# Eight stores of prepared W_out sums, begun on ScalarE's DMA queue in place of SyncE's

## The chip, the cores and the metric

The kernel runs on one core of one Trainium2 chip. The metric is the device time of one execution in microseconds (us); lower is better. A core has TensorE (PE, matrix products), VectorE (DVE), ScalarE (ACT), GpSimd (POOL) and SyncE (SP, which only begins transfers and waits). Each engine takes its own instructions strictly in order; between engines they wait on semaphores. A transfer is begun by an instruction of an engine and then runs by itself.

## The reference, cut to what matters

One decoder layer on a prompt of 2048 tokens and on 8 single decode tokens, all in float32:

```
h = rmsnorm(x, norm_g)
rq, rk, rv, rg, hq, hf, hi, hgate = split(h @ w_in, 8)      # 1024 -> 8 x 512
rq, rk = rotary(rq), rotary(rk) * 128**-0.5                 # 4 retention heads of 128
o_ret, s_ret = chunked_decay_recurrence(rq, rk, rv, log_gamma, s_ret)
logf = logaddexp(log(lb), log1p(-lb) + log_sigmoid(hf))     # 4 HGRN2 heads of 128
kin  = (1 - lb) * sigmoid(-hf)
o_hg, s_hg = chunked_decay_recurrence(silu(hq), kin, hi, logf, s_hg)
o = concat(head_rmsnorm(o_ret) * silu(rg), head_rmsnorm(o_hg) * silu(hgate))
y = rmsnorm(x + o @ w_out)                                  # w_out: 1024 x 1024
```

Returned are y for prompt and decode tokens and all new states. The recurrence is S_t = diag(f_t) S_(t-1) + k_t v_t^T, o_t = S_t^T q_t.

## The kernel before, in words

**Number format.** A float32 product is made of three products of a shorter format: each operand is split into a high part h (a rounded copy, made on ACT, line 115) and a low part l (the rest, made on DVE, line 116), and PE adds h·h, h·l and l·h. `hi_lo` does the two steps; `split` (line 118) does them for a 128x1024 tile, into a tile of the tag `wh` and one of the tag `wl`, of which there are three buffers each. Weights of `w_in` (w0, w1, ... in the order of use) and the sums of `w_out` share these six buffers.

**Stages.** The first 572 us make six of the eight projections and the retention heads, with block products that need fewer multiplications (seven for eight). From there to about 860 us run eight units, one for each half of the prompt and each HGRN2 head: a unit's PE work is the projection to the forget gate (`pjfh`) and to the query (`pjqh`), line 1039, in segments of up to 512 tokens. Between those matmuls PE does the recurrence of the unit before: scores (`pah`, line 1273; `plh`), transposed keys (`pkh`, line 1118), state updates (`puh`), outputs (`poh`, `poth`). The last stage multiplies by `w_out`: four token blocks plainly, the rest with the seven-product form, which needs sums of blocks of `w_out`.

**The path from a query segment to the scores.** When `pjqh` of a segment is complete, ACT makes its sigmoid (`qsh`, line 1095), DVE multiplies (`qqh`, line 1096) and multiplies by the gate (line 1098); the score matmuls `pah` read the result. `pkh` is copied out of PSUM by ACT (`ksh`, line 1120).

**The prepared sums.** Four times, beside units 0, 1, 2 and 4, a row block of `w_out` is loaded (`t_load_raw`), four sums are made on DVE (`t_sum`, lines 1365 to 1371), two of them are stored as they are (`t_keep`), and the other two, side by side in a 128x1024 tile, are split (`t_spool`; tiles `wos0h`, `wos0l` to `wos3h`, `wos3l`) and both parts are stored to DRAM (`t_store`, line 1383). They are read back near 900 us. The places come from a list of fractions of a unit (lines 1445 to 1449).

**What sets the order.** PE's order is as written. The instructions of the other engines are put in order by the layer that builds the program, by its own estimate of when each can start; it also hands out the buffers of a tag, and a new tile waits for the last use of the buffer that it gets, a store out of it among them. Transfers of SP and ACT count on eight counters in turn (`DMAHW0` to `DMAHW7`), and one that takes a counter waits until the transfer before it on that counter has landed. All stores of line 1383 are begun by SP, as nearly all other loads and stores are; ACT begins one transfer in the program, near the end (line 1774).

The lines that begin the stores, and when (as fractions of a unit behind 0.35, 1.35, 2.35 and 4.35):

```
def t_store(k):
    for x, y in zip("hl", tspl[k]):
        sp.dma_start(t_dram[x][:, :, k], ...)
steps += [t_spool, t_keep, t_store]
for f, d in zip(steps, (0, 0.12, 0.18, 0.24, 0.3, 0.4, 0.42, 0.54)):
```

Of the kernel before, what the change touches and what calls it, by code (L numbers as in the profile page):

```python
# [10 lines left out]
F32 = mybir.dt.float32  # L11
# [30 lines left out]
def step_kernel(ctx, tc, a, out):  # L42
    nc = tc.nc
    pe, act, dve, pool, sp = nc.tensor, nc.scalar, nc.vector, nc.gpsimd, nc.sync
# [1300 lines left out]
    def collect(h, u):  # L1345
# [3 lines left out]
    t_dram = {  # L1349
        x: dr.tile([P, 2, 4, GW], F32, tag=f"t{x}", name=f"t_dram{x}") for x in "hlr"  # L1350
    }
# [28 lines left out]

    def t_store(k):
        for x, y in zip("hl", tspl[k]):
            sp.dma_start(t_dram[x][:, :, k], y.bitcast(F32).rearrange("p (a b) -> p a b", a=2))

    def d_norm():
        x = pools["tp"].tile([8 * NB, P], F32, tag="dgt", name="do", bufs=2)
# [605 lines left out]
```

## Time and profile before

| what | value |
|---|---|
| three runs | 1034.69, 1038.95, 1041.99 us; median 1038.95 |
| the profiled execution | 1036.22 us, of which its span is 1034.4 |
| granted TensorE clock | 0.999 |
| PE busy in the span | 1017.0 us (98%) |
| DVE, ACT, POOL busy | 746.1 (72%), 559.2 (54%), 128.7 (12%) us |
| PE busy from 575 to 830 us | 251.7 of 255 us |
| busy share of the DMA engines, 658 to 670 us | 0.79 |

The time that hangs on line 1383 lies between 590 and 745 us of the span. Rows of the time line give start, duration, engine, line, operation, output and inputs (buffer numbers left out), and in brackets how long the engine stood idle ahead of it and for whom. `SPq` and `ACTq` are rows of instructions that begin transfers; their duration is the time in which the engine is held, not that of the transfer.

### The profile page before, as it was taken

What the parts mean: (1) busy time and instruction counts of PE and PEld (TensorE: products, weight loads), DVE (VectorE), ACT (ScalarE), POOL (GpSimd) and SP (SyncE); (2) the same over time, 40 slices, a digit from 0 to 9 for tenths busy, and PEclk for the clock granted to TensorE, in tenths of its full rate; (3) what the DMA queues carried; (4) which work ended last, traced back from release to release, by engine and by line L of the source; (5) the groups of instructions that cost most, each with busy time, mean ns of one, the idle gap of its engine ahead of it and who ended that gap; (6) DMA issues with size and microseconds to landing.
All of it is one profiled execution on the core that took longest, in us unless ns stands there. A gap on an engine that the chain in (4) does not pass through costs nothing.

```text
span 1034.4 us, 21591 instructions
## 1 busy us (share of the span) xinstructions
PE 1017.0 (98%) x8359; PEld 843.5 (82%) x8359; DVE 746.1 (72%) x1387; ACT 559.2 (54%) x1233; POOL 128.7 (12%) x231
## 2 busy tenths in 40 slices
PE   8999999999999999999999999999999999999997
PEld 7777878887778888878888889798788877888775
DVE  6886676887666876666666767768778676667786
ACT  7863346644445765545554756666556465443242
POOL 0410001000000111111111200110012102312122
PEclk9999999999999999999999999999999999999999
DMA  8699999779998974486775696745784395576652
GB/s 292 218 332 335 336 327 318 267 252 321 318 335 296 376 245 156 163 266 220 239 247 175 229 331 226 244 136 195 231 263 136 118 380 196 177 274 210 236 169 102
DMA packets 151271, 255.63 MB, mean 247 GB/s; under 512 B 11424, under 2 KB 79280, under 8 KB 151040
## 3 DMA queue, kind: packets, MB, share of 16 engines
q1 hardware_dynamic: 143584, 229.22, 65.3%
q0 software_dynamic: 7440, 24.76, 6.2%
q8 instruction: 66, 1.08, 0.4%
q14 instruction: 37, 0.30, 0.1%
q10 hardware_dynamic: 144, 0.26, 0.1%
HBM read 166.51 MB, written 87.69 MB: 246 GB/s over the span
## 4 chain that ended last, share of the span: by engine, by line
PE 78%; DMA 11%; ACT 5%; DVE 3%; issue 1%; SPq 1%; POOL 0%; POOLq 0%; ACTq 0%; DVEq 0%
PE po L360 11%; PE pjfh L1039 7%; PE pjqh L1039 6%; PE py L1670 4%; DMA xn<-in_x_prompt 2%; PE plh L1255 2%; PE par L744 1%; PE pur L751 1%; PE por L757 1%; PE por L759 1%; DMA or<-o_dram 1%; DMA T3l<-ws1T 1%; DMA a_dram<-xr 1%; PE puh L1126 1%; PE poh L1142 1%
## 5 line engine op out<-in xcount | busy, mean ns | idle before, releaser
L1235 ACT ACTIVATE kepth<-kh 128x1024 f32<-128x1024 f32 x24 | 25.5, 1061 | 70.7 <-DVE kh L1225 70.7
L1039 PE MATMUL pjfh<-xh,w_h 128*128 128x512 f32 (+2 forms) x160 | 59.6, 372 | 0.8 <-ACT fxh L1087 0.8
L1039 PE MATMUL pjqh<-xh,w_h 128*128 128x512 f32 (+2 forms) x160 | 59.0, 369 | 0.0
L1039 PE MATMUL pjqh<-xh,w_l 128*128 128x512 f32 (+2 forms) x160 | 55.7, 348 | 0.0
L1039 PE MATMUL pjfh<-xh,w_l 128*128 128x512 f32 (+2 forms) x160 | 55.7, 348 | 0.0
L1039 PE MATMUL pjqh<-xl,w_h 128*128 128x512 f32 (+2 forms) x160 | 55.6, 348 | 0.0
L1039 PE MATMUL pjfh<-xl,w_h 128*128 128x512 f32 (+2 forms) x160 | 55.6, 348 | 0.0
L1225 DVE TENSOR_TENSOR kh<-kh,fph 128x512 f32<-128x512 f32 x48 | 33.3, 693 | 18.4 <-PE plh L1255 12.6
L116 DVE TENSOR_TENSOR ab_l<-xr,ab_h 128x512 fp32r<-128x512 f32 (+1 forms) x40 | 37.3, 952 | 5.8 <-ACT ab_h L115 5.8
L782 DVE SCALAR_TENSOR_TENSOR obr<-por,omr,rg 128x128 f32<-128x128 f32 x64 | 18.0, 343 | 32.4 <-POOL omr L774 30.1
L772 ACT ACTIVATE obr<-por 128x128 f32<-128x128 f32 x64 | 16.9, 278 | 43.8 <-PE por L759 41.5
L115 ACT ACTIVATE ab_h<-xr 128x512 fp32r<-128x512 f32 (+1 forms) x40 | 32.4, 841 | 12.5 <-DVE xr L313 12.5
L419 ACT ACTIVATE vo<-vo 128x512 f32<-128x512 f32 x32 | 20.1, 629 | 27.0 <-DVE vo L413 13.7
L1039 PEld LDWEIGHTS pjfh<-xh,w_h 128*128 128x128 f32 x160 | 30.2, 189 | 5.3 <-ACT fxh L1087 1.1
L1039 PEld LDWEIGHTS pjqh<-xh,w_h 128*128 128x128 f32 x160 | 30.4, 190 | 4.8 <-issue 1.2
L1039 PEld LDWEIGHTS pjqh<-xh,w_l 128*128 128x128 f32 x160 | 30.1, 188 | 4.1
L1039 PEld LDWEIGHTS pjfh<-xh,w_l 128*128 128x128 f32 x160 | 30.1, 188 | 4.1
L1228 DVE TENSOR_TENSOR qqh<-qqh,fph 128x512 f32<-128x512 f32 x48 | 32.8, 683 | 0.0
L1039 PEld LDWEIGHTS pjqh<-xl,w_h 128*128 128x128 f32 x160 | 30.2, 189 | 2.9
L1039 PEld LDWEIGHTS pjfh<-xl,w_h 128*128 128x128 f32 x160 | 30.2, 189 | 2.7
L313 DVE SCALAR_TENSOR_TENSOR xr<-xr,g_in,rb 128x256 f32<-128x256 f32 x64 | 27.1, 479 | 6.6 <-issue 4.1
L1670 PE MATMUL py<-woh,oc_h 128*128 128x512 f32 x64 | 26.7, 417 | 1.6 <-issue 1.6
(1840 smaller groups left out, 3371.4 us busy)
## 6 DMA issues: line engine op xcount, KB each, us to landing
xr<-a_dram SPq DMA_DIRECT2D x24, 512.0 KB, 5.6
S<-s_dram SPq DMA_DIRECT2D x24, 512.0 KB, 6.4
xn<-in_x_prompt SPq DMA_DIRECT2D x32, 256.0 KB, 3.6
xr<-in_x_t SPq DMA_DIRECT2D x16, 512.0 KB, 5.9
a_dram<-xr SPq DMA_DIRECT2D x16, 512.0 KB, 4.3
s_dram<-S SPq DMA_DIRECT2D x16, 512.0 KB
wgr<-in_w SPq DMA_DIRECT2D x16, 512.0 KB, 8.2
xr<-a_dram SPq DMA_DIRECT2D x32, 256.0 KB, 4.4
```

The lines of the kernel that those rows point to most:

```text
L115: act.activation(h, src, AF.Copy)
L116: dve.tensor_tensor(l, src, h.bitcast(F32), op=ALU.subtract)
L313: dve.scalar_tensor_tensor(r[:, k], r[:, k], g_in[:, kk : kk + 1], spread_to[i], op0=ALU.mult, op1=ALU.mult)
L360: pe.matmul(ps, xx, ww, start=(first and n == 0), stop=(last and n == 2), skip_group_check=more)
L419: act.activation(o, src, AF.Silu)
L782: dve.scalar_tensor_tensor(o[:, cc], po[:, h], ms[:, h : h + 1], rb_of[c, "g"][:, cc], op0=ALU.mult, op1=ALU.mult)
L1039: pe.matmul(ps, ww[:, kk], x[:, k, b0 : b0 + n], start=(k == 0 and i == 0), stop=(k == KT - 1 and i == 2),)
L1225: dve.tensor_tensor(kv[:, :, 0, :], kv[:, :, 0, :], two[:, :, 1:2].to_broadcast([P, nb, b]), op=ALU.mult)
L1228: dve.tensor_tensor(qv[:, :, 1, :], qv[:, :, 1, :], two[:, :, 0:1].to_broadcast([P, nb, b]), op=ALU.mult)
L1235: act.activation(ss[:, 512:], k[:, :HALF], AF.Copy)
L1255: pe.matmul(dst[32 * i : 32 * i + 32, c], kk, qq, start=True, stop=True)
L1670: pe.matmul(ps, o[:, kk], w[:, k % 4, i * 512 : (i + 1) * 512], start=(k == 0 and n == 0), stop=(k == KT - 1 and n == 2),)
```

## The change

The two stores of each prepared block are begun by ScalarE. Nothing that is computed changes, and the bytes moved are the same.

```
 def t_store(k):
     for x, y in zip("hl", tspl[k]):
-        sp.dma_start(t_dram[x][:, :, k], y.bitcast(F32).rearrange("p (a b) -> p a b", a=2))
+        act.dma_start(t_dram[x][:, :, k], y.bitcast(F32).rearrange("p (a b) -> p a b", a=2))
```

The building layer then places other instructions anew. PE's and POOL's order stays; ACT has eight rows more, SP eight fewer.

On ACT at the third pair (unit 2), before; `w7_h` is the high part of the weights that unit 3's query projection uses, and in brackets are the counters it waits for:

```order
L1095 ACTIVATE qsh02512_6842<-pjqh02_512_6767 128x256 [waits PE_49]
L115 ACTIVATE w7_h_6964<-wr7_6962 128x1024 [waits DMAHW7_49,DMAHW5_49,DVE_49]
L1120 ACTIVATE ksh010_6872<-pkh010_6867 128x512 [waits PE_49]
L1120 ACTIVATE ksh011_6885<-pkh011_6880 128x512 [waits PE_49]
L1095 ACTIVATE qsh02768_6887<-pjqh02_768_6846 128x264
```

The same place on ACT, with the change:

```order
L1095 ACTIVATE qsh02512_6842<-pjqh02_512_6767 128x256 [waits PE_49]
L1383 DMA t_dramh_5499<-wos2h_6831 256x1x512 [waits DMAHW1_49,Activation_49]
L1383 DMA t_draml_5500<-wos2l_6832 256x1x512 [waits DMAHW3_49,DVE_49]
L1120 ACTIVATE ksh010_6872<-pkh010_6867 128x512 [waits PE_49]
L1120 ACTIVATE ksh011_6885<-pkh011_6880 128x512 [waits PE_49]
L1095 ACTIVATE qsh02768_6887<-pjqh02_768_6846 128x264
L115 ACTIVATE w7_h_6964<-wr7_6962 128x1024 [waits DMAHW5_49,DMAHW2_49]
```

The copy to `w7_h` has gone from ahead of the last query sigmoid of the unit to behind it. Its buffer is another too: before it was that of `wos2h`, and its wait on `DMAHW7` is for the store `t_dramh<-wos2h`; now it is that of `w5_h`, and `DMAHW2` stands for the store of `w5_h` to DRAM, begun a unit earlier. The first store waits on ACT for the store of `w6_l` (`DMAHW1`), the second for a load of `xr` (`DMAHW3`) and for DVE's `wos2l`.

On DVE at the same place (difference; - before, + with the change):

```order
-L116 TENSOR_TENSOR w7_l_6965<-wr7_6962,w7_h_6964 128x1024
 L1216 TENSOR_TENSOR fph02_6894<-fph02_6894 128x64
-L1096 TENSOR_TENSOR qqh02_6420<-pjqh02_768_6846,qsh02768_6887 128x264
 L1216 TENSOR_TENSOR fph02_6894<-fph02_6894 128x32
-L1098 TENSOR_TENSOR qqh02_6420<-qqh02_6420,fh02_6418 128x256
-L1347 COPY dq_173<-qqh02_6420 128x8
 L1216 TENSOR_TENSOR fph02_6894<-fph02_6894 128x16
 L1216 TENSOR_TENSOR fph02_6894<-fph02_6894 128x8
 L1218 COPY dech02_6902<-fph02_6894 128x8
+L1096 TENSOR_TENSOR qqh02_6420<-pjqh02_768_6846,qsh02768_6887 128x264
+L1098 TENSOR_TENSOR qqh02_6420<-qqh02_6420,fh02_6418 128x256
+L1347 COPY dq_173<-qqh02_6420 128x8
```

The low part `w7_l` follows that last row now, ahead of line 1225. Units 0 and 1 change alike: the last query segment goes ahead of the copy of the next weights, on ACT and on DVE.

On ACT at the fourth pair (unit 4; difference):

```order
 L1319 ACTIVATE Ah_5664<-Abh03_7498 32x8x32 x2
+L1383 DMA t_dramh_5499<-wos3h_7895 256x1x512
 L1314 ACTIVATE Ah_5664<-plh035_7919 32x4x32 x4
 L1316 ACTIVATE Ah_5664<-plh035_7919 64x4x64 x2
-L1095 ACTIVATE qsh10512_7992<-pjqh10_512_7906 128x512
+L1383 DMA t_draml_5500<-wos3l_7896 256x1x512
 L1120 ACTIVATE ksh030_7983<-pkh030_7978 128x512
 L1120 ACTIVATE ksh031_7990<-pkh031_7985 128x512
+L1095 ACTIVATE qsh10512_7992<-pjqh10_512_7906 128x512
```

Here the query sigmoid goes back, behind both stores and both copies of `ksh`.

## The prediction

> **What bounds the kernel now.** I read the page's first part, then who PE waits for in the stretch of the stores, then the chain of waits there, then the time line engine by engine.
>
> ```profile
> PE 1017.0 (98%) x8359; PEld 843.5 (82%) x8359; DVE 746.1 (72%) x1387; ACT 559.2 (54%) x1233; POOL 128.7 (12%) x231
> ```
>
> PE is busy for 1017.0 of 1034.4 us. Only what fills a gap of PE, or opens one, moves the time. Its waits between 575 and 830 us, where the stores lie:
>
> ```profile
> PE pah L1273 <- DVE qqh L1098: 1.6, 1, 1.6
> PE pjfh L1039 <- ACT fxh L1087: 0.8, 1, 0.8
> ```
>
> One gap there is longer than a microsecond. The chain of waits names its cause:
>
> ```profile
> 659.50 6.49 DMA t_dramh<-wos2h
> 666.09 1.07 ACT w_h L115
> 667.19 1.23 DVE w_l L116
> ```
>
> A store of the changed line is on the chain, 6.49 us from issue to landing, because ACT's next weight copy takes the buffer that it empties. On ACT, with what is queued behind:
>
> ```profile
> 661.59 0.39 ACT L1095 ACTIVATE qsh<-pjqh 128x256 f32<-128x256 f32 x1
> 666.09 1.06 ACT L115 ACTIVATE w_h<-wr 128x1024 fp32r<-128x1024 f32 x1 [4.11 <-DMA t_dramh<-wos2h]
> 667.06 1.06 ACT L1120 ACTIVATE ksh<-pkh 128x512 f32<-128x512 f32 x2
> 668.01 0.39 ACT L1095 ACTIVATE qsh<-pjqh 128x264 f32<-128x264 f32 x1
> ```
>
> ACT stands for 4.11 us in front of `w7_h`; behind that copy wait two key copies and the last query sigmoid. DVE and PE follow:
>
> ```profile
> 660.89 1.22 DVE L116 TENSOR_TENSOR wos2l<-wot,wos2h 128x1024 fp32r<-128x1024 f32 x1
> 668.92 0.42 DVE L1098 TENSOR_TENSOR qqh<-qqh,fh 128x256 f32<-128x256 f32 x1
> 669.90 0.69 DVE L1225 TENSOR_TENSOR kh<-kh,fh 128x512 f32<-128x512 f32 x1
> ```
>
> ```profile
> 663.71 0.60 PE L1118 MATMUL pkh<-ident,kh 128*128 128x128 f32 x4
> 666.98 0.88 PE L1273 MATMUL pah<-qqh,kh 128*32 128x64 f32 x48
> 669.40 0.43 PE L1273 MATMUL pah<-qqh,kh 128*32 128x64 f32 x16 [1.55 <-DVE qqh L1098]
> 669.76 0.50 PE L1039 MATMUL pjfh<-xh,w_h 128*128 128x512 f32 x1
> ```
>
> `pah` does 48 of its 64 matmuls, waits for the last query segment, and the projection goes on 2.78 us after `pah` began (669.76 - 666.98). The same step in unit 1 finds its data there:
>
> ```profile
> 631.78 1.10 PE L1273 MATMUL pah<-qqh,kh 128*32 128x64 f32 x64
> 632.81 0.50 PE L1039 MATMUL pjfh<-xh,w_h 128*128 128x512 f32 x1
> ```
>
> That takes 632.81 - 631.78 = 1.03 us.
>
> **The third pair: the gap.** With the change ACT no longer has `w7_h` ahead of the query sigmoid, and `w7_h` has a buffer that does not wait for this store. In its place ACT begins the two stores. What an issue costs an engine:
>
> ```profile
> L1383 SPq DMA_DIRECT2D t_draml<-wos2l x1: 729/729/729, 662.1 to 662.1; - x1
> L1383 SPq DMA_DIRECT2D t_dramh<-wos3h x1: 519/519/519, 731.9 to 731.9; - x1
> L1774 ACTq DMA_DIRECT2D out_y_prompt<-xro x1: 395/395/395, 1030.9 to 1030.9; - x1
> L156 SPq DMA_DIRECT2D w_h<-w_kepth x8: 332/864/4045, 668.9 to 789.1; - x8
> ```
>
> The same stores held SP 0.52 to 0.73 us; ACT's only issue, half as large, 0.40. The last row is the upper bound: an issue can hold SP 4.05 us, though that was a load. I take 0.52 for each, from the same stores, and 0.73 where the queue is busy, as here. The second store needs `wos2l`, ready at 660.89 + 1.22 = 662.11, and the `xr` load that had its counter before:
>
> ```profile
> 650.99 0.33 SPq L173 DMA_DIRECT2D w_keptl<-w_l  x1
> 652.21 7.08 SPq L186 DMA_DIRECT2D xr<-a_dram  x4
> ```
>
> ```profile
> xr<-a_dram SPq DMA_DIRECT2D x32, 256.0 KB, 4.4
> ```
>
> That is the first of the four loads, begun at 652.21; with 4.4 us it lands near 656.6, with the 6.49 of the slow store at 658.7. The first store's counter was held by the store of `w6_l`, begun at 650.99, which is gone sooner still. So on the clock of the old trace ACT is free at 661.59 + 0.39 = 661.98, has begun both stores by 661.98 + 2 x 0.73 = 663.44, copies the second keys after 663.71 + 0.60 = 664.31 until 664.9, and ends the sigmoid (0.39) at 665.3. In the old trace line 1098 ended (668.92 + 0.42 = 669.34) 0.94 us after its sigmoid (668.40); now that is 666.24. PE needs it at 666.98 + 0.88 = 667.86. The margin is 1.6 us, `pah` runs through in 1.03 instead of 2.78, and PE gains **1.75 us** (at the least the 1.55 in brackets).
>
> What is late next? `w7_h` runs from 665.3 to 666.4, and `w7_l` (1.23) on DVE until about 667.6, ahead of line 1225. That line waits for the end of `pah`, at 666.98 + 1.03 = 668.0, so 0.4 us of cover is left; without it line 1225 would start later by what is missing, as would the scores behind it. SP loses a wait and gets one:
>
> ```profile
> 668.86 0.41 SPq L156 DMA_DIRECT2D w_h<-w_kepth  x1
> ```
>
> This load now waits on SP for the store begun on ACT, about 662.5 + 6.49 = 669.0, and holds the value loads behind it as long as before. I cost that at nothing.
>
> **The fourth pair: a cost.** Here ACT's query sigmoid goes back.
>
> ```profile
> 733.38 1.11 ACT L1314 ACTIVATE Ah<-plh 32x128 f32<-32x128 f32 x4
> 734.50 0.77 ACT L1316 ACTIVATE Ah<-plh 64x256 f32<-64x256 f32 x2
> 735.99 0.60 ACT L1095 ACTIVATE qsh<-pjqh 128x512 f32<-128x512 f32 x1 [0.72 <-PE pjqh L1039]
> 736.49 1.08 ACT L1120 ACTIVATE ksh<-pkh 128x512 f32<-128x512 f32 x2
> ```
>
> ```profile
> 737.35 0.69 DVE L1098 TENSOR_TENSOR qqh<-qqh,fh 128x512 f32<-128x512 f32 x1
> ```
>
> ```profile
> 703.42 0.39 SPq L156 DMA_DIRECT2D w_l<-w_keptl  x1
> 703.86 0.42 SPq L1066 DMA_DIRECT2D v<-v_dram  x1
> ```
>
> ```profile
> 739.51 1.10 PE L1273 MATMUL pah<-qqh,kh 128*32 128x64 f32 x64
> ```
>
> The loads whose counters the two stores take were begun near 703.4 and 703.9, 30 us earlier. The first store moves line 1316's end from 735.27 to 735.79, the second lasts until 736.31; the key copies end between 737.4 and 737.6, the sigmoid 0.60 later, at 738.0 to 738.2. Line 1098 ended 1.45 us after it (738.04 - 736.59), so now at 739.45 to 739.65, while `pah` is due at 739.51. That is between nothing and 0.15 us; I take 0.05. All cover is used up here: each further microsecond that ACT is held costs PE one. With the upper bound of 4.05 for one of the issues the loss is 3.5 us.
>
> **The first two pairs.** At unit 0 the sigmoid stood behind a weight copy of a microsecond, which it now has behind it, with the stores in its place.
>
> ```profile
> 598.69 0.51 ACT L1089 ACTIVATE kh<-fxh,lb 128x264 f32<-128x264 f32 x1
> 600.60 0.37 ACT L1095 ACTIVATE qsh<-pjqh 128x264 f32<-128x264 f32 x1
> ```
>
> Two issues from 599.20 end at 600.24, so it is not later than the old 600.60. At unit 1 the second store waits on ACT for `wos1l`, and the key copies and the sigmoid wait behind it:
>
> ```profile
> 627.19 1.23 DVE L116 TENSOR_TENSOR wos1l<-wot,wos1h 128x1024 fp32r<-128x1024 f32 x1 [0.54 <-ACT wos1h L115]
> 629.74 0.38 ACT L1095 ACTIVATE qsh<-pjqh 128x264 f32<-128x264 f32 x1
> ```
>
> The store ends at 628.42 + 0.52 = 628.94, the key copies (1.08) at 630.0, the sigmoid at 630.4 instead of 630.12. The low part of the weights, which DVE did ahead of the query, now follows it, so `pah` at 631.78 still finds its query. Both pairs count as nothing, with 0.3 us either way.
>
> **The sum.** -1.75 + 0.05 = -1.7 us. The profiled execution took 1036.22 us (span 1034.4), which gives 1034.5. The median of the three runs is 1038.95, 2.7 above that execution, and they spread from 1034.69 to 1041.99. From the median I predict **1037.2 us**, 0.16% faster. A change of about 1% is what a measurement of this kernel can tell from none.
>
> **The rivals.** *The gain is given back* (chance 0.22). PE comes to 670 us earlier, but a later wait grows by as much: the 0.8 us for `fxh`, or one in the last stage that hangs on a transfer and not on PE. Against it: between 670 and 830 us PE has only small gaps. The time is 1036.2 on the profile, 1038.95 as a median. The Trainium skill (DMA: Bandwidth & Descriptors, Issuing engines are not separate DMA queues) says that transfers begun by several engines interleave on the same 16 DMA engines, and that only issue time on the sequencer is saved. By that rule alone the change would bring nothing, since SP's issue time bounds nothing here; the trace neither shows nor denies it, having hardly a transfer of ACT's. My gain does not rest on faster stores: it comes from what no longer stands behind one.
>
> *ScalarE is held while it begins a store* (0.10). Place: the fourth pair. If one issue there takes the 4.05 us of SP's longest, PE waits 3.5 us and the result is -1.75 + 3.5 = +1.8: 1040.7, slower than before. It turns the sign from 1.7 us of extra holding on. At the third pair the first 1.6 us are free. Against it: these very stores never took over 0.73 on SP.
>
> *More is gained* (0.10). SP is free of eight issues, the loads behind them start sooner, and the 0.8 us wait for `fxh` goes too: -1.75 - 0.84 = -2.6, so 1036.4.
>
> **How the numbers follow.** The forecast has the remaining 0.58. The cases give 1036.4 to 1040.7; the runs shown scatter by 4.3 below and 3.0 above their median, more than the cases differ, and a new median moves with them. So 1033 to 1042 should hold it. No case comes near 1%; only scatter or something unseen could: faster 0.03, within 1% 0.94, slower 0.03.
>
> **What would show it.** Right: in unit 2 no idle time ahead of `pah`, all 64 in one row, ACT's `w_h` behind `qsh` without a wait for `t_dramh<-wos2h`, and two ACTq rows of 0.4 to 0.75 us. At unit 4 `pah` waits at most 0.2 us for line 1098. Wrong: ACTq rows of more than a microsecond, a wait of `pah` for line 1098 in unit 4, or a longer wait of PE near 700 or 855 us.

## The result, and the profile after

The changed kernel took 1037.24 us and the kernel before 1039.78 us beside it (medians of 22 and 21 runs); the ratio is 0.9977, with a 95% interval of 0.9968 to 0.9987. By the prediction's bound of 1% that is no change; by the interval it is 1.3 to 3.3 us faster. Two further sets, of 11 and 12 runs, gave 0.9977 (0.9961 to 0.9993) and 0.9992 (0.9976 to 1.0009). Forecast were 1037.2 us and a gain of 1.7 us, a ratio of 0.9983, which all three intervals hold. Left out everywhere are four runs of 1440 to 3579 us: one of before, two of the fourth pair in halves, and one of the changed kernel's second set, the profiled one, at a granted clock of 0.655 from end to end, so that this profile isn't read.

The profiled execution of the change was the longest of its 22 (1041.4 us, span 1039.6), that of before one of the shorter (1036.22, span 1034.4). Their spans can't be set against each other; what can is the start of the same PE instruction in both. By how much it is later in the changed kernel is called the lag here. It is 2.6 to 2.7 us from 560 to 608 us (lost in the part before), a constant 2.00 us from 611 to 667, 0.24 us at 669 and 0.20 from 674 to 727. At the third pair the changed kernel has gained 1.76 us; at 610 us it has gained 0.63.

The page, first part, of the changed kernel, and who PE waits for longest between 575 and 830 us (total, times, longest):

```profile
PE 1020.8 (98%) x8359; PEld 845.4 (81%) x8359; DVE 747.7 (72%) x1387; ACT 559.5 (54%) x1233; POOL 129.1 (12%) x231
```

```profile
PE pjfh L1039 <- issue: 2.2, 1, 2.2
PE pjfh L1039 <- ACT fxh L1087: 0.8, 1, 0.8
```

The wait of `pah` for line 1098 is gone, the 0.8 us for `fxh` stands as before, and a stop of 2.2 us is new, in which PE waits for nothing that the profile shows. The time line of the changed kernel at the third pair, ACT first, then DVE and PE:

```profile
662.63 0.52 ACTq L1383 DMA_DIRECT2D t_dramh<-wos2h  x1
664.14 0.52 ACTq L1383 DMA_DIRECT2D t_draml<-wos2l  x1
...
666.84 0.39 ACT L1095 ACTIVATE qsh<-pjqh 128x264 f32<-128x264 f32 x1
667.11 1.06 ACT L115 ACTIVATE w_h<-wr 128x1024 fp32r<-128x1024 f32 x1
```

```profile
667.73 0.43 DVE L1098 TENSOR_TENSOR qqh<-qqh,fh 128x256 f32<-128x256 f32 x1
670.14 0.69 DVE L1225 TENSOR_TENSOR kh<-kh,fh 128x512 f32<-128x512 f32 x1 [0.71 <-PE pah L1273]
```

```profile
668.97 1.10 PE L1273 MATMUL pah<-qqh,kh 128*32 128x64 f32 x64
670.00 0.50 PE L1039 MATMUL pjfh<-xh,w_h 128*128 128x512 f32 x1
```

`w_h` (the tile `w7_h` of the order above) stands behind the query sigmoid and has no bracket: it waited for nothing. Line 1098 ends at 668.16, 0.8 us before `pah` begins, and all 64 matmuls are one row: 1.03 us from `pah` to the projection, where there were 2.78. The fourth pair, ACT and then PE:

```profile
731.92 0.52 ACTq L1383 DMA_DIRECT2D t_dramh<-wos3h  x1
...
733.38 0.55 ACT L1314 ACTIVATE Ah<-plh 32x128 f32<-32x128 f32 x2
733.72 0.52 ACTq L1383 DMA_DIRECT2D t_draml<-wos3l  x1
...
734.50 0.77 ACT L1316 ACTIVATE Ah<-plh 64x256 f32<-64x256 f32 x2
736.43 1.09 ACT L1120 ACTIVATE ksh<-pkh 128x512 f32<-128x512 f32 x2 [1.16 <-PE pkh L1118]
737.41 0.60 ACT L1095 ACTIVATE qsh<-pjqh 128x512 f32<-128x512 f32 x1
```

```profile
739.51 1.10 PE L1273 MATMUL pah<-qqh,kh 128*32 128x64 f32 x64
```

`pah` isn't delayed. Lines 1314 and 1316 start at 733.38 and 734.50 as in the trace of before: an issue of 0.52 us stands on ACT's queue at the same time as an activation, and moves none. Then the new stop, with what follows it on PE:

```profile
752.80 0.50 PE L1039 MATMUL pjfh<-xh,w_l 128*128 128x512 f32 x1 [2.16 <-issue]
...
753.79 0.63 PE L1144 MATMUL poh<-sth,qqh 128*128 128x128 f32 x2
```

Pairs of `poh` take 0.63 us here and 0.39 elsewhere: the granted clock is 0.50 for 3.4 us behind the stop (from 753.35). Between 748 and 760 us the lag grows by 4.0 us.

Open after this trace were two things: whether the third pair is the whole cause, and whether the stop at 752 us belongs to the change.

### The profile page after: what moved, and what is told of

It reads as the page before. It is cut to its first block, busy times and chain, and to the rows that moved or that the text cites. A ratio compares the mean times of both kernels' runs of the same rounds, so it can differ in the third digit from the quotient of the medians.

```text
span 1039.6 us, 21590 instructions
## 1 busy us (share of the span) xinstructions
PE 1020.8 (98%) x8359; PEld 845.4 (81%) x8359; DVE 747.7 (72%) x1387; ACT 559.5 (54%) x1233; POOL 129.1 (12%) x231
## 4 chain that ended last, share of the span: by engine, by line
PE 77%; DMA 12%; DVE 5%; ACT 3%; issue 2%; SPq 1%; POOL 0%; POOLq 0%; ACTq 0%; DVEq 0%
PE po L360 11%; PE pjfh L1039 8%; PE pjqh L1039 7%; PE py L1670 4%; DMA wgr<-in_w 2%; PE plh L1255 2%; PE pur L751 1%; PE por L757 1%; DMA T3l<-ws1T 1%; PE poh L1142 1%; DMA xn<-in_x_prompt 1%; DMA or<-o_dram 1%; PE por L759 1%; PE par L744 1%; PE puh L1126 1%
## 5 line engine op out<-in xcount | busy, mean ns | idle before, releaser
L1670 PE MATMUL py<-wol,oc_h 128*128 128x512 f32 x64 | 25.2, 394 | 2.9 <-issue 2.1
```

What stands on the lines that cost most here:

```text
L1670: pe.matmul(ps, o[:, kk], w[:, k % 4, i * 512 : (i + 1) * 512], start=(k == 0 and n == 0), stop=(k == KT - 1 and n == 2),)
```

## The experiments

**The third pair alone.**

```
-            sp.dma_start(t_dram[x][:, :, k], ...)
+            (act if k == 2 else sp).dma_start(t_dram[x][:, :, k], ...)
```

> Only the third pair's stores are begun on ScalarE. Theory (the gain is the weight copy that no longer stands in front of the query sigmoid at the third pair): the 64 matmuls of pah in unit 2 stand in one row with no idle time ahead of line 1098, 1.75 us are gained, ratio to before 0.9983 (0.9975 to 0.9990). Rival 1 (part of the gain comes from the other pairs, the trace of the changed kernel showed about 0.7 us at unit 0 and 0.2 near 700 us): the ratio is 0.7 to 0.9 us worse than that of the whole change, and unit 0 keeps its idle row of 0.45 us ahead of plh. Rival 2 (the gain is SyncE's freed queue): ratio about 0.9995.

Ratio 0.9971 (0.9954 to 0.9987), median 1036.37 us: better than the 0.9975 to 0.9990 expected, most of which the interval holds. Instructions at 680 us begin 1.79 us sooner against those at 640 than in the trace of before. PE's longest waits in the trace of the third pair alone, 575 to 830 us, have no `pah`:

```profile
PE pjfh L1039 <- ACT fxh L1087: 0.8, 1, 0.8
PE plh L1255 <- issue: 0.8, 1, 0.8
```

The third pair's stores bring at least what all eight do; rival 1 falls as far as the time goes, though its mark in the trace is there (a stop ahead of `plh` in unit 0, here of 0.75 us). Rival 2's 0.9995 lies outside the interval. There is no stop at 752 us.

**All pairs but the third.**

```
+            (sp if k == 2 else act).dma_start(t_dram[x][:, :, k], ...)
```

> The first, second and fourth pair's stores are begun on ScalarE, the third pair's on SyncE as before. Theory: the weight copy of unit 2 again waits about 4 us for the first store, pah stands 1.5 us for line 1098, and the ratio is 1.000 (0.999 to 1.0005). Rival 1: 0.7 to 0.9 us are gained without the third pair, ratio 0.9992, and the 0.45 us idle ahead of plh in unit 0 is gone. Rival 2 (SyncE's freed queue): about three quarters of the gain, ratio 0.9983.

Ratio 0.9991 (0.9977 to 1.0005), median 1038.84 us. The gap is back, on ACT and on PE in the trace of this kernel:

```profile
665.83 1.06 ACT L115 ACTIVATE w_h<-wr 128x1024 fp32r<-128x1024 f32 x1 [3.96 <-DMA t_dramh<-wos2h]
```

```profile
669.14 0.43 PE L1273 MATMUL pah<-qqh,kh 128*32 128x64 f32 x16 [1.39 <-DVE qqh L1098]
```

At the third pair the theory holds in the trace. Rival 1's mark is there as well: the 0.45 us ahead of `plh` in unit 0 is gone, and from 605 to 680 us this kernel gains 0.7 us on the trace of before; by 870 us it has lost 1.3 again. The interval holds nothing gained and also rival 1's 0.9992, so the time alone doesn't decide about the other three pairs.

**Another queue, but the old place of the copy.**

```
+            pool.dma_start(t_dram[x][:, :, k], ...)
```

> All eight stores are begun on GpSimd's queue; in the third pair the next weight copy still takes the buffer that the first store empties, and stands ahead of the query sigmoid. Theory (what counts is the place of the copy and its buffer, not which queue begins the store): the wait of the copy stays at 3.5 to 5 us, pah waits 1 to 2.5 us for line 1098, ratio 0.9995 to 1.001. Rival (a queue of its own makes the store faster, or SyncE freed is the gain): the store takes under 4.5 us, pah waits under 0.5 us, ratio about 0.9983.

Ratio 1.0037 (1.0018 to 1.0057): 3.8 us slower. In the trace with GpSimd's queue, first the store with its median time to landing, then ACT, then PE:

```profile
t_dramh<-wos2h POOLq DMA_DIRECT2D x1, 512.0 KB, 7.9
```

```profile
667.09 1.06 ACT L115 ACTIVATE w_h<-wr 128x1024 fp32r<-128x1024 f32 x1 [5.84 <-issue]
```

```profile
670.26 0.43 PE L1273 MATMUL pah<-qqh,kh 128*32 128x64 f32 x16 [3.14 <-DVE qqh L1098]
...
671.71 0.63 PE L1039 MATMUL pjfh<-xh,w_h 128*128 128x512 f32 x1
```

The bracket of the copy names no releaser, but the copy starts when the store has landed (659.15 + 7.9 = 667.05). SyncE is rid of all eight issues here, and nothing is gained: what counts is where the copy stands and what it waits for. The direction was as the theory had it, the sizes were not. The store landed 7.9 us after its start (6.49 from SyncE), `pah` waited 3.14 us instead of the 1 to 2.5 expected, and from 660 to 680 us the kernel loses 3.18 us, twice the 1.59 by which the wait grew (3.14 - 1.55). The other half is the matmuls of 0.63 us: as behind the stop at 752 us, the clock is low.

**The same gap closed without ScalarE.** The third sum is split into its own two blocks, so that the weight copy takes a free buffer:

```
-        tspl[k] = split(traw[k][0]..., f"wos{k}")
+        if k == 2:
+            r, h = (traw[k][n]... for n in range(2))
+            tspl[k] = (h.bitcast(F32R), r.bitcast(F32R))
+            hi_lo(*tspl[k], r)
```

> All stores stay on SyncE; the third sum is split within its own two blocks instead of into two of the six buffers shared with the weights, so the next weight copy waits for no store. Theory: the gap of 1.55 us ahead of pah in unit 2 goes without ScalarE beginning anything, ratio 0.9983 (0.9975 to 0.9990). Rival (the gain needs the stores off SyncE): pah runs through, but as much is lost later at a transfer behind the stores, or the gap stays; ratio about 1.000.

Ratio 0.9983 (0.9967 to 0.9999). `pah` on PE in the trace of this kernel:

```profile
669.53 1.10 PE L1273 MATMUL pah<-qqh,kh 128*32 128x64 f32 x64
```

The gap is gone with every store on SyncE, and the time falls as forecast for the change. The trace gains 1.29 us there and not 1.75, because `poth` in the same unit now waits 0.57 us for DVE.

**The changed kernel again.**

> The changed kernel once more, unaltered, beside the next three. Theory: ratio to before 0.9978 (0.9967 to 0.9988); the stop of 2.2 us in the middle of pjfh near 752 us, with a lower granted clock, was chance and is not there again; at unit 0 idle time ahead of plh (0 to 1.3 us in the five profiles so far) comes by chance and says nothing of the change. Rival: the stop near 752 us comes back, and is a cost of the fourth pair.

Ratio 0.9977 (0.9961 to 0.9993); for the stop see the third set, below.

**What an issue on ScalarE costs: the fourth pair in halves, and in quarters.**

```
+            y = y.bitcast(F32).rearrange("p (a b) -> p a b", a=2)
+            for p, n in ((0, P),) if k < 3 else ((r, 64) for r in range(0, P, 64)):   # quarters: 32
+                act.dma_start(t_dram[x][p : p + n, :, k], y[p : p + n])
```

> As the changed kernel, but the fourth pair is stored in halves: four issues on ScalarE in place of two. Theory A (ScalarE's sequencer begins a transfer while its activations run, so an issue costs only where the next activation already waits): L1314 and L1316 stand where they stood, the issues end about 0.8 to 1.3 us later than in the changed kernel, before the second key copy can start, and pah in unit 4 waits at most 0.2 us; ratio to the changed kernel 1.000. Theory B (as the prediction counted: each issue holds ScalarE for 0.4 to 0.52 us): the query sigmoid ends 0.8 to 1.0 us later and pah waits 0.6 to 1.0 us for line 1098; ratio to the changed kernel 1.0008.

> As the changed kernel, but the fourth pair is stored in quarters: eight issues on ScalarE. Now the first low quarter takes the counter of the first high quarter, and two others those of high quarters begun just before. Expected by both theories: ScalarE stands for their landing (4.5 to 6.5 us after their start near 732 to 735) until 739 to 741 us, the key copies and the query sigmoid come behind it, pah in unit 4 waits 2 to 4 us for line 1098, ratio to the changed kernel 1.002 to 1.004. This is the rival of the prediction (ScalarE is held) made on purpose. If the counters do not hold it, theory A expects 0.3 to 0.8 us and theory B 3 us.

Halves: ratio to before 0.9985 (0.9970 to 1.0000), that of the changed kernel beside it 0.9977. ACT and PE in the trace with halves:

```profile
729.36 0.53 ACTq L1385 DMA_DIRECT2D t_dramh<-wos3h  x1
...
729.98 0.56 ACTq L1385 DMA_DIRECT2D t_draml<-wos3l  x1
730.19 0.77 ACT L1316 ACTIVATE Ah<-plh 64x256 f32<-64x256 f32 x2
730.59 0.62 ACTq L1385 DMA_DIRECT2D t_draml<-wos3l  x1
732.11 1.09 ACT L1120 ACTIVATE ksh<-pkh 128x512 f32<-128x512 f32 x2 [1.15 <-PE pkh L1118]
```

```profile
735.19 1.10 PE L1273 MATMUL pah<-qqh,kh 128*32 128x64 f32 x64
```

Three issues stand beside the activations of lines 1314 and 1316 and end at 731.21; the key copy that follows waits for PE until 732.11 anyway, and `pah` doesn't wait. That is theory A in the trace; B's wait of 0.6 to 1.0 us isn't there. The times can't decide: the two ratios differ by 0.0008, which is B's figure, but each is known to 0.0015 only. Quarters: ratio 1.0074 (1.0055 to 1.0093), 7.7 us slower, where 1.002 to 1.004 was expected. ACT in the trace with quarters, and PE's wait:

```profile
735.04 9.95 ACTq L1385 DMA_DIRECT2D t_draml<-wos3l  x4
745.03 1.08 ACT L1120 ACTIVATE ksh<-pkh 128x512 f32<-128x512 f32 x2 [10.36 <-DMA t_draml<-wos3l]
```

```profile
PE pah L1273 <- DVE qqh L1098: 8.7, 1, 8.7
```

Here ScalarE is held, for 9.95 us, and not by the work of issuing but by the issues' counters. In the trace the second, third and fourth low quarter begin at 737.59, 740.10 and 744.43 us, each 0.02 us after the last signal of the transfer that had its counter before (737.57, 740.08 and 744.41). For the second and third that is a high quarter, as expected; for the last it is a value load that SyncE began only at 736.97, which the expectation of 739 to 741 us had left out. The lag grows by 11.8 us at `pah`, 3.1 more than the wait, and again the matmuls behind it run at a low clock.

**All four sums in place, stores on ScalarE.**

```
-        tspl[k] = split(traw[k][0]..., f"wos{k}")
+        r, h = (traw[k][n]... for n in range(2))
+        tspl[k] = (h.bitcast(F32R), r.bitcast(F32R))
+        hi_lo(*tspl[k], r)
...
+            act.dma_start(t_dram[x][:, :, k], ...)
```

> All four sums are split in place and all stores are begun on ScalarE: no weight copy waits for a store of the sums at any pair, and SyncE has eight issues fewer. Theory: only the third pair had a gap, so the ratio to before is that of the change, 0.9975 to 0.9988. Rival (freed buffers let weights be loaded earlier and give more): 0.996 or less.

Ratio 1.0000 (0.9989 to 1.0011), so both expectations fail. PE's waits in the trace of all four in place, the largest:

```profile
PE py L1672 <- issue: 2.5, 1, 2.5
PE pjfh L1039 <- issue: 1.3, 1, 1.3
...
PE poth L1164 <- DVE obh L1157: 0.8, 2, 0.6
```

The third pair gives 1.29 us as in the other kernel that splits in place. The stop near 750 us then takes 1.5, and about 860 us another 3.2 go: a stop of 2.50 us ahead of the last stage's first matmuls (1.62 before) and a low clock behind it. A gain can be lost again at these stops; nothing else in the trace has grown as much.

**Does the stop near 750 us belong to the change?** The changed kernel and the third pair alone once more, side by side:

> The changed kernel once more, for its profile beside the next. SyncE's loads of unit 4 start earlier there than before (724.5 us in place of 734), and the traffic near 750 us is denser. Theory: the third pair gives its 1.75 us, and a stop of PE near 752 us (2.2 us in the first profile) comes in some executions only; ratio to before 0.9978 (0.9967 to 0.9988), with or without it. Rival (the fourth pair brings the stop every time): it is there again with 1 to 2.5 us, and the third pair alone, in the next run, is 0.5 to 2 us faster than this one.

> Only the third pair on ScalarE, a second time. Theory: the third pair is all there is, so the ratio to before is 0.9983 (0.9970 to 0.9990), the same as the whole change within 0.0010. Rival (the fourth pair costs up to 2 us in some executions): the ratio is 0.0005 to 0.0020 better than that of the whole change, and no stop near 752 us.

Ratios 0.9992 (0.9976 to 1.0009) and 0.9986 (0.9971 to 1.0001), medians 1037.41 and 1036.20 us. PE in the trace of the changed kernel, then of the third pair alone:

```profile
748.68 0.50 PE L1039 MATMUL pjfh<-xh,w_l 128*128 128x512 f32 x1 [1.00 <-issue]
857.57 0.80 PE L1670 MATMUL py<-wol,oc_h 128*128 128x512 f32 x1 [2.07 <-issue]
```

```profile
857.15 0.50 PE L1670 MATMUL py<-wol,oc_h 128*128 128x512 f32 x1 [0.99 <-issue]
```

The stop is there again, and not with the third pair alone. The two kernels' times can't be told apart for certain: the means of all runs are 1037.04 (45 runs) and 1036.66 us (24), a difference of 0.4 us with 1.0 either way, the medians 1.1 us apart. All profiles together, three places at which PE stops with no releaser (us):

| kernel | ahead of `plh`, 610 us | in `pjfh`, 750 us | ahead of `py`, 857 us |
|---|---|---|---|
| before | 0.45 | 0 | 1.62 |
| third pair alone, twice | 0.75, 0.83 | 0, 0 | 1.26, 0.99 |
| third in place, stores on SyncE | 1.33 | 0 | 1.14 |
| the change, twice | 0, 0 | 2.16, 1.00 | 2.11, 2.07 |
| all but the third | 0 | 0 | 1.96 |
| GpSimd's queue | 0 | 1.38 | 2.28 |
| all in place, on ScalarE | 0 | 1.28 | 2.50 |
| fourth in halves | 0 | 0 | 1.28 |
| the two with longer sigmoids, below | 0, 0.64 | 0.27, 0.45 | 2.20, 2.65 |

With the other pairs on SyncE (the first four profiles) the means are 0.84, 0 and 1.25 us, with them elsewhere (eight) 0.08, 0.82 and 2.13. The quarters are left out: they had 0.62 us at the first place, and PE was held ahead of the two others. So in these profiles moving those pairs takes about 0.8 us off the first stop and puts about 0.8 and 0.9 on the others; single profiles scatter widely (0 to 2.16 at 750 us), and no run moves one of those pairs alone.

**How a stop of PE is paid for.** The query sigmoid of unit 4's last segment is made several times over, so that PE has to wait:

```
+            for _ in range(3 if (name, t0) == ("h10", 512) else 1):      # long: 6
                 act.activation(sg[:, :n], ps, AF.Sigmoid)
```

> The changed kernel, in which ScalarE makes the query sigmoid of unit 4's last segment three times over instead of once (the same values): PE is made to wait for it at pah. Each further one takes 0.60 to 0.75 us, so pah waits 1.1 to 1.5 us for line 1098. Both theories: the time grows by that wait alone, the matmuls behind it take 0.39 us as before; ratio to the changed kernel 1.0012 (1.000 to 1.0025).

> As the last, with the sigmoid made six times over: pah waits 2.9 to 3.7 us. Theory (a stop of PE of more than about 2.1 us also lowers the granted clock for some 4 us behind it, as behind the stops of 2.16, 2.28, 2.50, 3.14 and 8.7 us in the profiles so far, and not behind those of 1.1 to 2.11 us): the matmuls of pjfh behind pah take 0.63 us in place of 0.39, and the time grows by 1.5 to 2 us more than the wait, 4.5 to 5.5 us in all; ratio to the changed kernel 1.0045 to 1.0055. Rival (the time grows by the wait alone): 2.9 to 3.7 us, ratio 1.003, matmuls of 0.39 us.

Short: ratio to before 1.0000 (0.9983 to 1.0017); long: 1.0010 (0.9991 to 1.0029); the changed kernel beside them 0.9992. PE in the trace with three sigmoids, then with six:

```profile
737.57 0.65 PE L1274 MATMUL pah<-qqh,kh 128*32 128x64 f32 x32 [0.70 <-DVE qqh L1099]
...
738.95 0.40 PE L1039 MATMUL pjfh<-xh,w_h 128*128 128x512 f32 x1
...
740.45 0.48 PE L1039 MATMUL pjfh<-xh,w_h 128*128 128x512 f32 x1
```

```profile
741.55 0.65 PE L1274 MATMUL pah<-qqh,kh 128*32 128x64 f32 x32 [2.58 <-DVE qqh L1099]
...
743.58 0.63 PE L1039 MATMUL pjfh<-xh,w_h 128*128 128x512 f32 x1
...
746.00 0.48 PE L1039 MATMUL pjfh<-xh,w_h 128*128 128x512 f32 x1
```

From the second half of `pah` to the same matmul of the next projection are 740.45 - 737.57 = 2.88 us behind the short stop and 746.00 - 741.55 = 4.45 behind the long one: 1.57 us for the clock, as the theory expected. The waits were shorter than expected (0.70 and 2.58 us). In the runs' times the long stop costs less than in its profile, which was that of the longest of its 12 runs: the mean is 2.9 us above that of all runs of the changed kernel, with 1.7 either way, where wait and clock make 2.58 + 1.57 = 4.15 in the trace. The wait alone would lie within that too, so between rival and theory the times don't decide; the matmuls of the trace do, for that execution.

## Why the prediction was right, step by step

**The gap at the third pair** went as worked out. Forecast -1.75, measured 1.76 (the change), 1.79 (alone), with all else moved and this left about none (0.2). Set back by the lag of 2.00 us, the second store's issue ends at 662.66 (forecast 663.44), the sigmoid at 665.23 (665.3), line 1098 at 666.16 (666.24), the low part of the weights at 667.44 (667.6). Nothing was late next: line 1225 waits for `pah`, as its bracket of 0.71 shows. The issue cost was sized too high (0.73, measured 0.52), which changed nothing. That the time itself, 1037.24, meets the forecast 1037.2 so closely is luck: the kernel before had 1039.78 and not the 1038.95 from which the sum set out, and the medians differ by 2.5 us and not by 1.7.

**SyncE's lost and new wait** cost nothing, as forecast, but came sooner than worked out (669.0 us for the load of the kept weights). In the trace of the change:

```profile
669.33 0.33 SPq L156 DMA_DIRECT2D w_h<-w_kepth  x1
```

It waits 3.2 us on SyncE for the first store. On the clock of before it begins at 667.33, since the store began beside line 1314's activations, at 660.63 on that clock, and not behind the sigmoid. The first value load behind it begins when it did (672.07 - 2.00 = 670.07; before, 670.08).

**The fourth pair** cost nothing at `pah`; forecast were 0.05 and at most 0.15. The sigmoid ends at 738.01 (forecast 738.0 to 738.2) and line 1098 at 739.46, but the reason given was wrong in two places. "The first store moves line 1316's end from 735.27 to 735.79" failed: that line ends where it ended, since issues go beside activations. The sigmoid is later because the key copies stand ahead of it. And "each further microsecond that ACT is held costs PE one" failed by 0.56 us: two further sigmoids of 0.63 us made PE wait 0.70. The first 32 matmuls of `pah` don't need the last segment, a cover that the forecast counted at the third pair and forgot here. What the pair moves elsewhere was not in the forecast: SyncE, rid of its stores, begins a state load (`dS`) at 724.52 us instead of 733.75, and from 748 to 752 us, where the new stop is, the DMA engines have a share of 1.05 instead of 0.87.

**The first two pairs** count as nothing at `pah`, as forecast; on PE in the trace of the change both have their 64 matmuls in one row:

```profile
605.07 1.10 PE L1273 MATMUL pah<-qqh,kh 128*32 128x64 f32 x64
...
633.77 1.10 PE L1273 MATMUL pah<-qqh,kh 128*32 128x64 f32 x64
```

What happened at 610 us, 0.63 us gained, was not in the forecast.

**The rivals.** ScalarE held by an issue: no issue of whole or half stores took over 0.63 us; it was held where the issues' counters were still in use, in the quarters. More is gained: no, the 0.8 us for `fxh` is in every trace. The gain is given back: this has a part of the truth. The forecast looked for it at a wait for a transfer; what grows are stops of PE at 750 and 857 us that the profile gives no releaser, while the 610 us stop shrinks, in the kernels that move the other pairs. One sign of being wrong that the prediction named did come, a longer wait of PE near 855 us (2.11 and 2.07 us in the traces of the change, 1.62 before); the forecast put such stops at nothing. Together the three come to about +0.9 us in the profiles, without the clock. From 605 us to the end, the gap included, the two profiles of the change lose 2.5 and 1.6 us on that of before, and the two of the third pair alone gain 2.3 and 0.8. That of before was a short execution, though, and in the times the two kernels can't be told apart. So the sum of -1.7 came out within the measurement, but not every part of it was known, and how much of the third pair's gain the other pairs cost on average stays open.

## What to carry to other kernels

When an engine stands for a transfer, look at which instruction stands first in its queue and which buffer that one takes; here the remedy was that a weight copy no longer stood ahead of what PE needed, and it worked as well by splitting one tile in place with the stores left where they were. Beginning a transfer on ScalarE was nearly free here while its counter was free, and very dear when it wasn't. Before moving many transfers for the sake of one place, try the one alone: the others shift the traffic, and with it stops for which the profile names no cause.

## What the runs showed of the hardware that was not expected

**PE stops at fixed places of its program, and waits there for its own instructions.** In the thirteen traces that are read, every stop of PE over 0.2 us for which the profile names no releaser stands behind 6849, 11457, 12481 or 14785 instructions of PE (matmuls, weight loads and sequencer rows). The differences are 4608, 1024 and 2304, which are 18, 4 and 9 times 256; the stops behind 12481, near 784 us, are short (0.2 to 0.3 us). Two of the stops lie in these stretches of the trace of the change (the last two columns are the busy share of the DMA engines and GB/s):

```profile
748.00:752.00 4.00, 2.64 (x134) 1.00 1.05 368
855.00:860.00 5.00, 4.24 (x100) 1.00 1.09 339
```

In the trace of before the first of them has 0.87 and 247 GB/s, and no stop. The Trainium skill (Runtime: NRT & Kernel Launch, Instruction fetch mechanics) says that an engine's instructions are fetched by transfers in blocks of 256 and that crossing a block is mostly hidden. The spacing agrees with it. Hidden it was not: the stops took up to 2.65 us. The traces hold these transfers too, as one line of the page of each of the thirteen (packets, MB, share):

```profile
q8 instruction: 66, 1.08, 0.4%
```

The 66 packets have 16,384 bytes each, and PE's 16,842 instructions make 65.8 blocks of 256. All 29 stops end 1.2 to 1.6 us after the end of the packet of the block that begins there. Of the 816 other block borders in these traces, PE passes 8 within 1.6 us of their packet, with at most 0.2 us of idle time, and all others later. At 11457 instructions the packet runs from 747.37 to 748.25 us in the trace of before, and PE passes at 750.02; in that of the change, where PE is no later until then, it runs from 750.51 to 751.39, and PE goes on at 752.80. So PE waits for its instructions. The packet isn't slower (0.88 us in both), it begins later; that the kernel's own transfers hold it up fits the shares above, but no run took them away to show it.

**A stop of two microseconds or more can halve the clock behind it.** Stretches of the trace with six sigmoids behind the stop of 2.58 us, then one of the other behind its 0.70 us; the columns are the stretch, its length, PE busy with its instructions, granted clock, share of the DMA engines, GB/s:

```profile
742.55:745.05 2.50, 2.50 (x7) 0.50 1.03 309
745.55:749.55 4.00, 4.00 (x25) 1.00 0.95 346
```

```profile
738.15:742.15 4.00, 4.00 (x29) 1.00 1.02 304
```

The clock is 0.50 for 3.4 us, which costs about 1.6 us. It fell so behind stops of 2.07, 2.16, 2.28, 2.50, 2.58, 2.65, 3.14 and 8.7 us (for 10.2 us behind the last), and not behind 1.55, 1.96, 2.11 or 2.20. The Trainium skill (TensorE: Matmul & The Clock Gate, HAM oscillation — how this bites in real kernels) tells to avoid idle gaps of more than about 3.4 us. The half clock is what it describes; as a bound for a stop, 3.4 us is too long here, 2.07 was enough. The gap of 1.55 us that the change removed was shorter than any of these: no low clock stood behind it, and it was worth 1.76 us, little more than its length. At 3.14 us, with GpSimd's queue, the added 1.6 us cost 3.2.
